# Attention scores of a transformer block: the keys' lo products on all 128 rows for short key ranges

## The chip, the cores and the metric

One core of a Trainium2 chip runs one program with a single launch. The metric is the device time of the program in microseconds, as the median of several runs. The engines of the core work side by side, each through its own queue in order: TensorE (PE, matmuls; PEld is its weight load), VectorE (DVE), ScalarE (ACT), GpSimd (POOL) and SyncE (SP, here for DMA alone).

## The reference, cut to what matters

The reference is one layer of a transformer block over 1024 tokens with a model width of 1024: a norm, a mixer of two attention branches (A and B), a second norm and a mixture of 32 experts. All of it is float32. The change touches the attention scores, of which there are three that matter here, all with head width 64 and eight query heads:

```python
s = einsum('bthd,btkd->bthk', q, ks) * scale        # branch A: 256 selected keys per query, one key head
s = einsum('btkgd,btksd->btkgs', qr, ks) * scale    # branch B, selected blocks: two key heads
s = einsum('btkgd,bskd->btkgs', qr, kw) * scale     # branch B, window of 512 keys
p = masked_softmax(s, mask)
```

Sixteen blocks of 64 keys are chosen out of sixteen in the second one, so it is causal attention over all keys. The kernel computes the first one over all causal keys too, with a bias that masks what isn't selected.

## The kernel before, in words

The kernel works in stages one behind another: norm and projections, with the index scores and their top 256 (0 to 474 us), attention (474 to 812), the merge and output projection with the router, and the experts with the final norm (both together 812 to 1429).

**Operands.** The score matmuls take operands of the type fp32r, so each float32 operand is split into a hi part and a lo part (the value minus its hi part). Of a query tile of 128 tokens, `q` holds for every head the 64 rows of the hi part and the 64 rows of the lo part in the 128 partitions: hi in partitions 0 to 63 and lo in 64 to 127 for a head of place x = 0, the other way round for x = 1 (lines 603 to 611). The keys `kk` hold the hi part (index 0) and the lo part (index 1), each twice: in partitions 0 to 63 and again in 64 to 127 (lines 620 to 635).

**A stage** (`stage`, line 896) is one query tile i of one of the three branches: selected blocks (`slc`), window and A. Its key range is n = (i - j0 + 1) x 128 keys; j0 is 0, in the window stage max(0, i - 4). There are 24 stages and eight small ones for compressed keys (`cmp_stage`). The query tiles go in the order 2, 3, 7, 6, 5, 1, 4, 0 (line 67).

**The scores of a pair of heads** (`score(h)`, for h and h + 1 as x = 0 and 1) go into PSUM tiles `s2` (in the trace `s`): one for both heads if n is at most 512, one for each otherwise, with two buffers. A range over 512 is cut in two: at 384 if n is 640, else at 512. The *first products* (line 929) multiply the 128 partitions of `q` by the hi part of the keys: hi x hi plus lo x hi at once. The *second products* (line 935) add hi x lo: for x = 0 they take partitions 0 to 63 of `q` and of the lo keys, for x = 1 partitions 64 to 127. They are half the array each, on different rows of it, and the loop puts the two heads side by side for each cut. `behind` (line 868) adds an ordering edge, without a semaphore, so that each of these matmuls comes right in the order written; the first of the second products stands behind the last of the first ones.

**What follows a pair.** VectorE adds the mask, negates and takes the row minimum (lines 944, 945, 952), ScalarE makes the exponential with its sum (953), VectorE the reciprocal (956) and POOL the scaling (960). In the next stage's time, `product(j)` turns the probabilities by PE transposes (971), VectorE or ScalarE copies them out (866), and `av` multiplies them by the values (879, 883): two matmuls of 64 output partitions side by side, half of the array's columns each.

**The order.** The loop at line 1058 issues the scores of a stage between the products of the stage before it. The program is scheduled by a planner (line 1692, `schedule_with_timeline_sim=True`): it places each engine's instructions by its own estimate of times, within the data dependencies and the edges added by hand.

Of the kernel before, what the change touches and what calls it, by code (L numbers as in the profile page):

```python
# [20 lines left out]
P = 128  # L21
# [80 lines left out]
def emit(tc, A):  # L102
# [366 lines left out]
    with ExitStack() as pi:  # L469
# [8 lines left out]
        def keys(g):  # L478

            ts_ = slice(g, g + G)  # L480
            src = kraw[:, ts_].rearrange("p t (a b) -> p t a b", a=2)
            out = ip.tile(tb, F32, name="qr")
            dve.tensor_tensor(ra, src, cos[:, ts_, None, ::2].to_broadcast(tb), op=OP.mult)
            dve.tensor_tensor(rb, src, sin[:, ts_, None, ::2].to_broadcast(tb), op=OP.mult)
            dve.tensor_tensor(out[:, :, 0], ra[:, :, 0], rb[:, :, 1], op=OP.subtract)
            dve.tensor_tensor(out[:, :, 1], ra[:, :, 1], rb[:, :, 0], op=OP.add)
            ks = ip.tile([P, G, 2, 2, 32], F32R, name="ks")
            kb = out.rearrange("p t a b -> p t (a b)")
            for x in range(2):
                act.activation(ks[:, :, x, 0], kb, AF.Copy)  # L490
            for x in range(2):
                dve.tensor_tensor(ks[:, :, x, 1], kb, f32(ks[:, :, x, 0]), op=OP.subtract)

            def turn():
                tr = ps1.tile([P, 512], F32, name="tr", bufs=2)
                for t in range(G):
                    pe.transpose(r32(tr[:, t * P:(t + 1) * P]), ks[:, t].rearrange("p a b c -> p (a b c)"), identr)
                dve.tensor_copy(kist[:, g * P:(g + G) * P], tr)
            return turn
# [188 lines left out]
    with ExitStack() as pk:  # L688
# [6 lines left out]
        with ExitStack() as pt:  # L695
# [77 lines left out]
            for t in range(2, NT):  # L773
                n = (t + 1) * P
# [14 lines left out]
            with tc.If(fv > 0):  # L789
                for t in range(2, NT):  # L790
                    n = (t + 1) * P
# [38 lines left out]
    with ExitStack() as pa:  # L830
# [32 lines left out]
        def flat(tr, n):  # L863
            ev[0] += 1
            h = ap_.tile([P, 512], F32, name="pth", bufs=NPT)
            return h[:n], (act.copy if EV[ev[0] % len(EV)] else dve.tensor_copy)(h[:n], tr[:n])  # L866

        def behind(i, j, sync=False):

            cl = mybir.DependencyClass  # L870
            tc.add_manual_dep(i.ins, j.ins.name, mybir.DependencyInfo(cl.Sync if sync else cl.NoSync, mybir.DependencyReason.DATA),
                              reason="side by side")
# [14 lines left out]
        def place(h):  # L887

            return h // 4 * 4 + h % 2 * 2 + h % 4 // 2
# [6 lines left out]
        def stage(i, q, keys, j0, gate, masked, vidx, avf, first, last, win=False):  # L896

            n = (i - j0 + 1) * P

            fold = win and i >= 4 and FOLD  # L900
            n_ = n - P if fold else n
            pgs = {}
            st = {}

            def score(h):

                g, hh = divmod(h, 4)
                if hh == 0:
                    st[g] = (ap_.tile([P, 4], F32, name="nm", bufs=4), ap_.tile([P, 4], F32, name="sm_", bufs=4))
                nm, sm_ = st[g]  # L910
                kk = keys(h)

                cut = 384 if n == 640 else 512
                s2s = []
                for x in range(2):

                    if n_ > 512 or x == 0:
                        pg = ap_.tile([P, S], F32, name="pg", bufs=NPG)
                    if n > 512 or x == 0:
                        s2 = ps2.tile([P, 1024], F32, name="s2", bufs=2)  # L920
                    o_ = 512 * x if n <= 512 else 0
                    p0 = 512 * x if n_ <= 512 else 0
                    pgs[h + x] = pg[:, p0:p0 + n_]
                    s2s.append(s2[:, 512 - cut + o_:])
                cs = [(c, w_) for c, w_ in ((0, min(n, cut)), (cut, n - cut)) if w_ > 0]
                mm = None
                for x in range(2):
                    for c, w_ in cs:
                        mm_, mm = mm, pe.matmul(s2s[x][:, c:c + w_], q()[:, place(h + x)], kk[:, 0, j0 * P + c:j0 * P + c + w_], start=True, stop=False)
                        if mm_:  # L930
                            behind(mm, mm_)
                for c, w_ in cs:
                    for x in range(2):
                        r = slice(64 * x, 64 * x + 64)
                        mm_, mm = mm, pe.matmul(s2s[x][:, c:c + w_], q()[r, place(h + x)], kk[r, 1, j0 * P + c:j0 * P + c + w_], start=False, stop=True)
                        behind(mm, mm_)

                mask = bias[:, soff[i]:soff[i] + n] if masked else window if win and i >= 4 else causal[:, S - n:]
                if fold:
                    fr = ap_.tile([P, 2, P], F32, name="fr", bufs=1)  # L940
                    nf = ap_.tile([P, 2], F32, name="nf", bufs=2)
                    for x in range(2):
                        y = hh + x
                        dve.tensor_tensor_reduce(fr[:, x], s2s[x][:, :P], mask[:, :P], -1.0, 3e38, op0=OP.add, op1=OP.min, accum_out=nf[:, x:x + 1])
                        dve.tensor_tensor_reduce(pgs[h + x], s2s[x][:, P:n], mask[:, P:], -1.0, 3e38, op0=OP.add, op1=OP.min, accum_out=nm[:, y:y + 1])
                        dg = pgs[h + x][:, n_ - P:]
                        dve.tensor_tensor(dg, dg, fr[:, x], op=OP.min)
                    dve.tensor_tensor(nm[:, hh:hh + 2], nm[:, hh:hh + 2], nf, op=OP.min)
                for x in range(2):
                    pg, y = pgs[h + x], hh + x  # L950
                    if not fold:
                        dve.tensor_tensor_reduce(pg, s2s[x][:, :n], mask, -1.0, 3e38, op0=OP.add, op1=OP.min, accum_out=nm[:, y:y + 1])  # L952
                    act.activation(pg, pg, AF.Exp, bias=nm[:, y:y + 1], scale=-1.0, accum_out=sm_[:, y:y + 1])  # L953
                if h % NB == NB - 2:
                    hb = hh - NB + 2
                    dve.reciprocal(sm_[:, hb:hh + 2], sm_[:, hb:hh + 2])
                    for x in range(NB):
                        h_ = h - NB + 2 + x
                        g2 = 1.0 if gate is None else gat[:, i, gate * 8 + h_:gate * 8 + h_ + 1]
                        pool.tensor_scalar(pgs[h_], pgs[h_], sm_[:, hb + x:hb + x + 1], g2, op0=OP.mult, op1=OP.mult)  # L960

            def product(j):
                pts = []
                both = fold and j == i

                def transposes():
                    c = n_ - (i - j + 1) * P
                    for g in range(2):
                        tr = ps2.tile([P, 512], F32, name="tr", bufs=3)
                        for hh in range(4):  # L970
                            pe.transpose(tr[:, hh * P:(hh + 1) * P], pgs[4 * g + hh][:, c:c + P], ident)  # L971
                        if both:
                            for x in range(2):
                                h = ap_.tile([P, 512], F32, name="pth", bufs=NPT)
                                pts.append((h, dve.tensor_tensor(
                                    h.rearrange("p (a q) -> p a q", a=4), tr.rearrange("p (a q) -> p a q", a=4),
                                    parts[:, x:x + 1].to_broadcast([P, 4, P]), op=OP.mult)))
                        else:
                            pts.append(flat(tr, P))

                def matmuls():
                    if both:
                        av(avf(), lambda g: vidx(g, j0), pts[1::2], False, False)
                        av(avf(), lambda g: vidx(g, j), pts[::2], False, last)
                    else:
                        av(avf(), lambda g: vidx(g, j), pts, first and j == j0, last and j == i)
                return transposes, matmuls, pts

            return ([lambda h=h: score(h) for h in range(0, 8, 2)], [product(j) for j in range(j0 + (1 if fold else 0), i + 1)])

        def cmp_stage(i, q, avf):
# [704 lines left out]
```

## Time and profile before

| | |
|---|---|
| median of 3 runs | 1431.48 us (1431.32 to 1436.68) |
| profiled execution | 1430.88 us |
| its span, first to last instruction | 1429.0 us |
| PE busy | 1332.3 us, 93% of the span |
| VectorE busy | 939.4 us, 66% |
| ScalarE busy | 700.6 us, 49% |
| POOL busy | 492.2 us, 34% |
| mean granted TensorE clock | 0.972 |

Busy times of matmuls overlap, since a matmul begins before the one ahead of it has left the array, and their ends are modelled. What one matmul costs its queue is read from the distance between two starts.

### The profile page before, as it was taken

How to read it: one execution, taken by the hardware profiler on the slowest of the kernel's cores; microseconds unless marked ns; L12 is line 12 of the kernel's file. 1: busy time of each engine (PE TensorE's matmuls, PEld its weight loads, DVE VectorE, ACT ScalarE, POOL GpSimd, SP SyncE). 2: the span in 40 equal slices, each digit the busy share in tenths (PEclk: the TensorE clock that was granted, in tenths of full speed). 3: DMA queues.
4: the chain of work that ended last, by engine and by line, in shares of the span. 5: the costliest groups of instructions: out<-in, count | busy, mean ns of one | idle time of the engine just before them, and what ended most of it. 6: DMA issues, size and time to landing. Idle time of an engine off the chain costs nothing. (4 is left out here: it accounts for less than half of the span.)

```text
span 1429.0 us, 21436 instructions
## 1 busy us (share of the span) xinstructions
PE 1332.3 (93%) x7095; PEld 999.3 (70%) x7095; DVE 939.4 (66%) x2335; ACT 700.6 (49%) x1452; POOL 492.2 (34%) x572
## 2 busy tenths in 40 slices
PE   4989999999999999999999999999689999898993
PEld 3889999988888655555565588877466667566662
DVE  7884778689600576677776696556766767565656
ACT  5513677622211575565576652222366656455554
POOL 3223777822312554444464400000132232233213
PEclk9999999999999999999999999999889999999996
DMA  6321443223333110101020274685689997699874
GB/s 202 80 63 59 143 131 107 79 83 103 91 94 111 45 53 8 45 16 30 19 72 16 60 230 140 197 305 180 221 292 296 326 325 237 199 327 316 300 235 179
DMA packets 126646, 214.82 MB, mean 150 GB/s; under 512 B 23081, under 2 KB 62033, under 8 KB 126530
## 3 DMA queue, kind: packets, MB, share of 16 engines
q1 hardware_dynamic: 110754, 174.53, 37.0%
q0 software_dynamic: 13680, 33.52, 8.6%
q10 hardware_dynamic: 2096, 5.36, 1.0%
q8 instruction: 57, 0.93, 0.3%
q14 instruction: 59, 0.48, 0.1%
HBM read 180.38 MB, written 49.28 MB: 161 GB/s over the span
## 5 line engine op out<-in xcount | busy, mean ns | idle before, releaser
L953 ACT ACTIVATE pg<-pg,nm 128x512 f32<-128x512 f32 (+7 forms) x192 | 138.9, 726 | 47.3 <-DVE nm L952 35.8
L221 PE MATMUL pj<-wh,hTl 128*128 128x288 f32 (+1 forms) x512 | 152.7, 299 | 7.8 <-DVE hTl L377 7.8
L219 PE MATMUL pj<-wh,hTh 128*128 128x288 f32 (+1 forms) x512 | 152.9, 299 | 1.9 <-DVE rb L260 1.0
L220 PE MATMUL pj<-wl,hTh 128*128 128x288 f32 (+1 forms) x512 | 152.0, 297 | 1.1 <-DVE wl L189 1.1
L189 POOL TENSOR_TENSOR wl<-wr,wh 128x512 fp32r<-128x512 f32 (+1 forms) x60 | 80.9, 1360 | 167.4 <-ACT wh L188 165.8
L971 PEld LDWEIGHTS tr<-ident,pg 128*128 128x128 f32 x784 | 84.9, 142 | 61.4 <-issue 30.3
L971 PE MATMUL tr<-ident,pg 128*128 128x128 f32 x784 | 115.6, 283 | 1.3 <-ACT pth L866 1.2
L220 PE MATMUL u<-gl,xh 128*128 128x512 f32 x256 | 112.6, 440 | 2.5 <-DVE gl L1432 2.5
L1471 POOL DMA_INDIRECT acc<-y,lis x30 | 55.7, 1858 | 161.0 <-ACT y L1465 106.9
L219 PE MATMUL u<-gh,xh 128*128 128x512 f32 x256 | 107.9, 422 | 2.2 <-ACT gh L1431 1.5
L221 PEld LDWEIGHTS pj<-wh,hTl 128*128 128x128 f32 x512 | 97.7, 191 | 9.6 <-DVE hTl L377 9.1
L221 PE MATMUL u<-gh,xl 128*128 128x512 f32 x256 | 103.3, 403 | 0.0
L1432 DVE TENSOR_TENSOR gl<-cr,gh 128x1024 fp32r<-128x1024 f32 x68 | 81.5, 1221 | 32.0 <-ACT gh L1431 24.3
L219 PE MATMUL pj<-hTh,wh 128*128 128x512 f32 x256 | 101.2, 395 | 0.0
L221 PE MATMUL pj<-hTh,wl 128*128 128x512 f32 x256 | 101.1, 395 | 0.0
L220 PE MATMUL pj<-hTl,wh 128*128 128x512 f32 x256 | 100.8, 394 | 0.0
L219 PEld LDWEIGHTS pj<-wh,hTh 128*128 128x128 f32 x512 | 98.1, 192 | 3.3 <-ACT hTh L376 1.3
L220 PEld LDWEIGHTS pj<-wl,hTh 128*128 128x128 f32 x512 | 97.8, 191 | 2.4 <-DVE wl L189 1.6
L866 DVE COPY pth<-tr 128x512 f32<-128x512 f32 (+1 forms) x102 | 69.8, 687 | 42.8 <-PE tr L971 36.1
L866 ACT COPY pth<-tr 128x512 f32<-128x512 f32 (+1 forms) x102 | 58.5, 580 | 66.2 <-PE tr L971 38.1
L1432 DVE TENSOR_TENSOR gl<-ck,gh 128x1024 fp32r<-128x1024 f32 x55 | 66.7, 1222 | 35.8 <-PE u L220 20.3
L1431 ACT ACTIVATE gh<-cr 128x1024 fp32r<-128x1024 f32 x68 | 70.2, 1062 | 17.4 <-DMA cr<-in_w_gate_up 8.2
(590 smaller groups left out, 3432.8 us busy)
## 6 DMA issues: line engine op xcount, KB each, us to landing
cr<-in_w_gate_up SPq DMA_DIRECT2D x68, 512.0 KB
ck<-in_w_gate_up SPq DMA_DIRECT2D x55, 512.0 KB
cr<-in_w_down SPq DMA_DIRECT2D x32, 512.0 KB
ck<-in_w_down SPq DMA_DIRECT2D x30, 512.0 KB
wr<-in_w_in SPq DMA_DIRECT2D x48, 256.0 KB
qscr<-qTs SPq DMA_DIRECT2D x96, 128.0 KB
q<-qscr POOLq DMA_DIRECT2D x24, 512.0 KB, 3.7
xt<-in_x SPq DMA_DIRECT2D x16, 512.0 KB
```

Source lines behind the costliest of these rows:

```text
L189: eng.tensor_tensor(lo[:, k:k + 2, w], raw[:, :, w], f32(hi[:, k:k + 2, w]), op=OP.subtract)
L219: pe.matmul(ps, lh, rh, start=first, stop=False)
L220: pe.matmul(ps, lh, rl, start=False, stop=False)
L221: pe.matmul(ps, ll, rh, start=False, stop=last)
L866: return h[:n], (act.copy if EV[ev[0] % len(EV)] else dve.tensor_copy)(h[:n], tr[:n])
L953: act.activation(pg, pg, AF.Exp, bias=nm[:, y:y + 1], scale=-1.0, accum_out=sm_[:, y:y + 1])
L971: pe.transpose(tr[:, hh * P:(hh + 1) * P], pgs[4 * g + hh][:, c:c + P], ident)
L1431: act.activation(gh, w, AF.Copy)
L1432: dve.tensor_tensor(gl, w, f32(gh), op=OP.subtract)
L1471: pool.indirect_dma_start(out=acc[:], out_offset=bass.IndirectOffsetOnAxis(ap=idx, axis=0), in_=y, in_offset=None, compute_op=OP.add, boun ...
```

## The change

For key ranges of at most 640 keys (five key tiles), the second products take all 128 partitions of `q` and of the lo keys. They compute hi x lo plus lo x lo, where before the lo x lo part was left out. They are full-array matmuls then, and the ordering edge ahead of each of them is left out. For n above 640 nothing is changed. The number of matmuls is the same.

```diff
+                short = n <= 640
                 for c, w_ in cs:
                     for x in range(2):
-                        r = slice(64 * x, 64 * x + 64)
+                        r = slice(0, P) if short else slice(64 * x, 64 * x + 64)
                         mm_, mm = mm, pe.matmul(s2s[x][:, c:c + w_], q()[r, place(h + x)], kk[r, 1, j0 * P + c:j0 * P + c + w_], start=False, stop=True)
-                        behind(mm, mm_)
+                        if not short:
+                            behind(mm, mm_)
```

## Rows read from the trace of the kernel before

**Rows 1.** Windows: stretch, busy us (x instructions) of PE, PEld, DVE, ACT, POOL; clock, DMA, GB/s.

```profile
474.00:486.00 12.00, 9.47 (x44) 5.35 (x44) 9.34 (x36) 10.27 (x29) 6.57 (x10) 0.89 0.14 45
...
715.00:738.00 23.00, 22.13 (x144) 14.36 (x143) 17.14 (x68) 18.50 (x62) 19.86 (x34) 1.00 0.27 83
...
787.00:812.00 25.00, 25.00 (x165) 15.56 (x165) 15.86 (x73) 16.34 (x60) 14.89 (x30) 1.00 0.09 24
...
1050.00:1400.00 350.00, 336.40 (x1360) 228.80 (x1358) 227.35 (x265) 201.91 (x295) 101.65 (x63) 0.99 0.87 287
```

**Rows 2.** PE's waits, 474 to 812 us: us in total, times, longest us.

```profile
PE s L929 <- DVE nm L952: 6.3, 9, 1.1
```

**Rows 3.** Timeline of PE, 512 keys: start us, us, engine, line, op, out<-in, shapes, xcount.

```profile
505.80 0.71 PE L929 MATMUL s<-kB,q 128*128 128x512 f32 x2
506.44 0.51 PE L935 MATMUL s<-kB,q 64*128 64x512 f32 x2
506.88 0.66 PE L971 MATMUL tr<-ident,pg 128*128 128x128 f32 x4
507.46 0.64 PE L879 MATMUL av<-pth,vB 128*64 128x512 f32 x1
```

**Rows 4.** Timeline of PE, 512 keys, transposes between first and second products.

```profile
500.09 0.71 PE L929 MATMUL s<-kB,q 128*128 128x512 f32 x2
500.64 0.60 PE L971 MATMUL tr<-ident,pg 128*128 128x128 f32 x4
501.17 0.50 PE L935 MATMUL s<-kB,q 64*128 64x512 f32 x2
```

**Rows 5.** Timeline of PE in the projections: full matmuls of 512 and of 256 columns.

```profile
400.35 0.39 PE L219 MATMUL pj<-hTh,wh 128*128 128x512 f32 x1
400.58 0.39 PE L220 MATMUL pj<-hTl,wh 128*128 128x512 f32 x1
...
451.93 0.28 PE L220 MATMUL pj<-wl,hTh 128*128 128x256 f32 x1
452.05 0.28 PE L221 MATMUL pj<-wh,hTl 128*128 128x256 f32 x1
```

**Rows 6.** Timeline of PE, 384 keys.

```profile
495.34 0.44 PE L935 MATMUL s<-kA,q 64*128 64x384 f32 x2
495.71 0.55 PE L971 MATMUL tr<-ident,pg 128*128 128x128 f32 x3
```

**Rows 7.** Timeline of PE, 256 keys.

```profile
719.13 0.38 PE L935 MATMUL s<-kB,q 64*128 64x256 f32 x2
719.45 0.44 PE L971 MATMUL tr<-ident,pg 128*128 128x128 f32 x2
```

**Rows 8.** Timeline of PE, 640 keys (384 and 256 columns, merged under the first shape).

```profile
743.39 0.83 PE L929 MATMUL s<-kB,q 128*128 128x384 f32 x4
744.15 0.56 PE L935 MATMUL s<-kB,q 64*128 64x384 f32 x4
744.64 0.66 PE L971 MATMUL tr<-ident,pg 128*128 128x128 f32 x4
```

**Rows 9.** Timeline of PE, 128 keys.

```profile
795.61 0.42 PE L929 MATMUL s<-kB,q 128*128 128x128 f32 x2
795.95 0.33 PE L935 MATMUL s<-kB,q 64*128 64x128 f32 x2
796.21 0.66 PE L971 MATMUL tr<-ident,pg 128*128 128x128 f32 x4
```

**Rows 10.** Timeline of PE, 512 keys, value products behind the pair.

```profile
503.09 0.50 PE L935 MATMUL s<-kB,q 64*128 64x512 f32 x2
503.52 0.64 PE L879 MATMUL av<-pth,vB 128*64 128x512 f32 x1
```

**Rows 11.** Timeline, 640 keys: [idle us before it <- releaser].

```profile
560.46 0.56 PE L929 MATMUL s<-kB,q 128*128 128x384 f32 x2 [0.58 <-DVE nm L952]
...
561.54 0.29 DVE L944 CUSTOM_DVE_ANT_0 fr<-s,window 128x128 f32<-128x128 f32 x1 [0.53 <-PE s L935]
```

## The prediction

> **What bounds the kernel now.** I read the page's engine table first: TensorE (PE) is the busiest engine by far, and the diff touches the attention stage alone (474 to 812 us), so I asked for the busy times of that stage cut at its query tiles. The reader is to see two kinds of stretch. In the last one, query tile 0, PE is busy 25.00 of 25 us while VectorE has 15.86 and POOL 14.89; in query tile 1 it is 22.13 of 23, with POOL close behind at 19.86. In the first one, PE is busy only 9.47 of 12 and VectorE 9.34 [rows 1]. A busy PE may still stand in a queue of its own, so the view of PE's waits comes next: over the whole stage its largest entry is 6.3 us for VectorE's row minimum, nine waits, because a new score tile must wait until VectorE has read the old one [rows 2]. Nothing else is large. So attention goes at the pace of TensorE's own instructions, except in a few places where VectorE sets it. The third view is the timeline of PE alone, read by the distance from one start to the next. The ends of matmuls are modelled; their starts give the slots.
>
> **What a pair costs today.** At four key tiles (512 keys) two first products start at 505.80, the half-array pair at 506.44, transposes at 506.88 and the next operation at 507.46 [rows 3]. So 0.64 us for two full products, 0.44 for the pair, 0.58 for four transposes. Elsewhere the same two full products are followed by transposes and not by half-array work: 500.09 to 500.64 is 0.55, and those four transposes take 0.53, to 501.17 [rows 4]. Hence entering the half-array pair costs 0.09 us, and coming back to transposes 0.05. A plain full product of 512 columns in a run takes 0.23 (400.35 to 400.58), one of 256 columns 0.12 (451.93 to 452.05) [rows 5]. The 0.55 is then 2 x 0.23 plus a lead of 0.09, which the first product has in both versions. The pair itself, 0.44, is hardly shorter than two plain products, 0.46: both halves start together, but nothing else runs beside them.
>
> **The change part by part.** It adds no DMA, no wait, no instruction. For n up to 640 the two second products of a head pair become full-array matmuls; 18 of the 24 stages are short, with four head pairs each, so 72 pairs: 12 each at 128, 256, 384 and 512 keys and 24 at 640 (window stages of tiles 5 to 7, all three of tile 4). Per pair followed by transposes, or by the next first products, the saving is: the entry (0.09), plus the pair minus the plain products that replace it, plus the return (0.05).
> - 512 keys: 0.09 + 0.44 - 0.46 + 0.05 = 0.12.
> - 384: the pair takes 0.37 [rows 6]. A plain product of 384 comes out of the 640 case, where four first products take 0.76 [rows 8]: less the lead and the entry, and less two of 256, 0.17 remain for each. 0.09 + 0.37 - 0.34 + 0.05 = 0.17.
> - 256: the pair takes 0.32 [rows 7]; 0.09 + 0.32 - 0.24 + 0.05 = 0.22.
> - 640: two pairs in a row take 0.49 (744.15 to 744.64) [rows 8] against 0.58 for four plain products; 0.09 - 0.09 + 0.05 = 0.05.
> - 128: 0.34 for the first products and 0.26 for the pair [rows 9]. A plain product of 128 in a run isn't shown. Taking lead and entry from the 0.34 leaves 0.08 each; 0.12 (the slot of 256) is the other end. Before is 0.34 + 0.26 + 0.05 = 0.65; after is 0.09 + 4 x 0.08 = 0.41 to 0.09 + 4 x 0.12 = 0.57: a saving of 0.08 to 0.24. I take a slot of 0.10, between the ends, and 0.16.
>
> Where the value products (av, half the columns, two side by side) follow, the entry and return don't go away, they move: the array must be regrouped for av anyhow, and the half-array pair hands over to av in the same 0.43 (503.09 to 503.52) [rows 10]. There only pair minus plain products is left: -0.02 at 512, +0.03 at 384, +0.08 at 256, -0.09 at 640, about +0.02 at 128. In the timeline nine pairs stand ahead of av: 2 at 512, 1 at 384, 1 at 256, 1 at 640, 4 at 128.
>
> Thirteen pairs stand where VectorE sets the pace or the clock is low: 7 at 384 at the start, where the granted clock is 0.89 of full over the stretch [rows 1], 1 at 256, 5 at 640. PE's saving there is worth between nothing (VectorE is late next) and the full 7 x 0.17 + 0.22 + 5 x 0.05 = 1.66; I take half, 0.83.
>
> The sum over the others: 128: 8 x 0.16 + 4 x 0.02 = 1.36; 256: 10 x 0.22 + 0.08 = 2.28; 384: 4 x 0.17 + 0.03 = 0.71; 512: 10 x 0.12 - 2 x 0.02 = 1.16; 640: 18 x 0.05 - 0.09 = 0.81. Together 6.32, with the paced ones 7.15, so 7.2 us. The ends of the 128 term (eight pairs by 0.08 either way) and of the paced pairs put it at 5.7 to 8.6.
>
> The ordering edges between second products go too. The planner then sets these matmuls where its own costs put them; the trace before cannot show that order. One more change of grouping around an av pair costs 0.14 (entry and return); one saved gains as much. With some fifteen moved either way that is 2 us to both sides; I take none.
>
> Does it reach the end? After attention PE is again the fullest engine: 336.40 of 350 us in the expert stage, where DMAs are busy 0.87 of the time [rows 1]. Those weight loads go into buffers that PE's work frees, so they begin earlier by the same amount; I count the saving whole. The profiled execution took 1430.88 us (1429.0 span and 1.9 around it), 0.6 below the median of the runs, 1431.48. From the median, 1431.5 - 7.2 = 1424.3.
>
> **A rule that speaks against it.** The trace shows 0.44 us for the lone pair at 512 [rows 3]. The Trainium skill, "TensorE: Matmul & The Clock Gate", Part 3 ("Measured speedup vs the span model"), says that matmuls on different row groups together last as long as one matmul plus some 4 ns for each further one. By that the pair would be worth 0.23, and the change would add a whole stream of columns for each pair, some 14 us in all; the lone pairs of this trace don't bear that out. It is the second rival below, there worked out from rows alone.
>
> **The rivals.**
> 1. *The saved time turns into waits.* In query tile 1 POOL is busy 19.86 of 23 us and PE would save 2.3 of them; at tiles 0 and 2 each stage is a short chain score, minimum, exponential, normalise, transpose. If VectorE, ScalarE or POOL catch up there, the 256 and half of the 128 terms are lost, 3 us: gain 4.2, so 1427.3. For it: the POOL row. Against it: PE 25.00 of 25 in tile 0 with all others under two thirds [rows 1].
> 2. *The cost of a pair is not the change of grouping.* Each pair has overhead beyond one stream of its columns: at 512, 0.09 + 0.44 - 0.23 + 0.05 = 0.35, at the other sizes much the same; 72 x 0.34 is 24.5 us. If it comes from the second product as such (adding to a PSUM tile just written), full-array products keep it, and the added streams must be paid: 12 x (0.10 + 0.12 + 0.17 + 0.23) + 24 x 0.29 = 14.4 us. With a quarter of the overhead gone it ends at 1431.5 + 14.4 - 6.1 = 1440. It decides for slower as soon as less than 0.6 of the overhead goes. Against it: first products that follow one another in one tile group show neither the 0.09 nor the 0.21 [rows 4, 5].
> 3. *More than the sum.* With the edges gone, the second product of head x = 0 no longer stands behind the first product of x = 1. Where the latter waits for its score tile, VectorE waits too: at 640 keys PE waited 0.58 us at 560.46 for x = 1, and VectorE then sat idle 0.53 until the half-array products ended [rows 11]. x = 0 could be ready before that. Given back at about half a microsecond in six or seven such places, this adds 3 us to the 7.2. In the first stretch, where PE stood idle a fifth of the time, the granted clock is 0.89; less idling might leave it at the upper of its two levels, 2.4 GHz, for longer. I put the whole at 10.5, 1421.
> 4. *It does nothing.* The planner takes the freed time for another order that loses as much: 1431.
>
> **How the numbers follow.** About 0.5%, 7.2 us, is what a measurement of this kernel can tell from no change, so faster is below 1424.3 and slower above 1438.6. The forecast, 1424.3 with its own range 1422 to 1427, has 0.50, and its lower half is faster by that bound: 0.25. Rival 1 has 0.17 (same), rival 2 0.08 (slower), rival 3 0.20 (faster), rival 4 0.05 (same). Faster 0.45, same 0.47, slower 0.08. The range that holds 8 in 10 runs from below rival 3 to past rival 4: 1416 to 1433; it leaves out rival 2 and the far end of rival 3.
>
> **What would show it.** In the changed timeline the four products of a head pair should take 0.09 + 4 x 0.23 = 1.01 at 512 keys instead of 1.08 (505.80 to 506.88 [rows 3]) and 0.57 at 256, and four transposes behind them 0.53 instead of 0.58. The half-array rows of the 72 pairs are gone, with starts 0.12 to 0.23 apart in their place. Attention should end some 7 us earlier with PE's waits unchanged. If the new starts are 0.2 or more apart at 256 columns, rival 2 is right; if slots shrink and the waits for VectorE or POOL grow, rival 1; if the waits for VectorE at 640 keys shrink, rival 3. The prediction is wrong if attention ends within 3 us of where it did, or more than 12 earlier.

## The result, and the profile after

The changed kernel takes 1407.89 us (median of 4 runs, 1407.07 to 1410.02) against 1431.97 (4 runs) for the kernel before: a ratio of 0.9827, 95% interval 0.9803 to 0.9851, or 24 us less. Forecast were 7.2 us less, 1424.3. Attention, from its first compressed product to the start of its last value product, went from 341.1 us (473.9 to 815.0) to 318.3 (473.6 to 791.9). That is nearly all of it: what follows attention takes 613.9 us before and 613.3 after.

The engine table of the changed kernel's page: TensorE's matmuls (PE) are less busy by 17.5 us and its weight loads (PEld) busier by 9.5; VectorE, ScalarE and POOL are within 1.5 us of where they were.

```profile
PE 1314.8 (94%) x7095; PEld 1008.8 (72%) x7095; DVE 939.7 (67%) x2335; ACT 699.1 (50%) x1452; POOL 492.9 (35%) x572
```

In the changed kernel the second products are line 937, the transposes 974, the row minima 947, 948 and 955. First the slots, from its timeline of PE: 512, 256 and 128 keys.

```profile
497.80 0.71 PE L929 MATMUL s<-kB,q 128*128 128x512 f32 x2
498.35 0.63 PE L937 MATMUL s<-kB,q 128*128 128x512 f32 x2
498.81 0.60 PE L974 MATMUL tr<-ident,pg 128*128 128x128 f32 x4
...
704.17 0.48 PE L929 MATMUL s<-kB,q 128*128 128x256 f32 x2
704.49 0.40 PE L937 MATMUL s<-kB,q 128*128 128x256 f32 x2
704.73 0.40 PE L929 MATMUL s<-kB,q 128*128 128x256 f32 x2
...
768.17 0.42 PE L929 MATMUL s<-kB,q 128*128 128x128 f32 x2
768.43 0.39 PE L937 MATMUL s<-kB,q 128*128 128x128 f32 x2
768.65 0.29 PE L974 MATMUL tr<-ident,pg 128*128 128x128 f32 x1
```

From start to start, the four products at 512 keys take 498.81 - 497.80 = 1.01, against 1.08 in [rows 3], and at 256 keys 0.56: the predicted 1.01 and 0.57. (A slot is the distance from one start to the next.) A full product of 128 columns has a slot of 0.22 / 2 = 0.11, where 0.10 was taken. So the pieces are as predicted. Yet the gain is three times their sum; what else has gone is in the waits and the clock.

PE's waits after, 474 to 812 us (us in total, times, longest us):

```profile
PE s L929 <- DVE nm L955: 3.0, 4, 1.1
...
PE s L929 <- DVE nm L948: 0.3, 1, 0.3
```

The first answers to [rows 2], 6.3 us in nine waits. The windows show where the waits were and a second thing that went with them. These are the kernel before and then the changed one (columns as in [rows 1]):

```profile
548.00:572.00 24.00, 20.48 (x94) 11.33 (x92) 15.31 (x50) 12.38 (x26) 12.18 (x12) 0.86 0.00 0
...
760.00:790.00 30.00, 27.51 (x170) 16.05 (x170) 21.32 (x73) 18.55 (x45) 11.34 (x15) 1.00 0.06 19
```

```profile
474.00:486.00 12.00, 8.97 (x50) 6.89 (x50) 9.97 (x38) 10.52 (x31) 6.99 (x11) 1.00 0.16 46
548.00:572.00 24.00, 23.74 (x148) 15.26 (x145) 19.63 (x63) 15.28 (x34) 11.68 (x13) 1.00 0.08 23
760.00:790.00 30.00, 30.00 (x202) 19.19 (x200) 19.77 (x82) 20.46 (x71) 16.00 (x32) 1.00 0.09 27
1026.00:1376.00 350.00, 335.93 (x1363) 228.25 (x1362) 227.74 (x264) 202.68 (x294) 101.26 (x63) 1.00 0.87 287
```

Between 548 and 572 us, PE was idle for 3.5 us of 24 and the granted clock was 0.86; after, it is idle for 0.26 and the clock is 1.00, and 148 matmuls stand where 94 did (not the same work, since the stages begin at other times). In the first stretch (474 to 486 us) the clock went from 0.89 [rows 1] to 1.00, though PE stood idle for 3.03 of the 12 us, against 2.53 before. The expert stage is unchanged against [rows 1] (335.93 for 336.40), only 24 us earlier.

To split the gain, every distance from one PE start to the next in attention was set against the median distance for the same operation, columns and neighbours over the traces of this case. The medians are "slots", what stands over them by more than 0.15 us is "waits", and the surplus in stretches at the 1.2 GHz level is "half clock". Between 0.8 and 3.2 us of small differences remain over, so the parts don't add up to the whole quite. Another way of taking the medians moves the first two columns by about 1 us, and waits against half clock by 2 us in the last row; the column "attention" is read from two starts and depends on no median. All in us, attention alone, from one profiled execution of each kernel. The last column counts how often PE goes from one grouping of the array to another (half-array second products, value products, all else). The rows between the first and the changed kernel, and the last one, are the experiments told below.

| kernel | slots | waits | half clock | attention | switches |
|---|---|---|---|---|---|
| before | 319.6 | 15.6 | 3.8 | 341.1 | 305 |
| full products, order of before held | 311.1 | 17.9 | 2.7 | 334.9 | 170 |
| half products, order of the next line held | 318.1 | 11.1 | 2.9 | 334.1 | 301 |
| full products, all edges kept | 309.6 | 12.9 | 0 | 325.7 | 167 |
| full, edges kept, head by head | 309.7 | 6.2 | 0 | 318.3 | 168 |
| changed kernel | 309.7 | 6.1 | 0 | 318.3 | 168 |
| half products, edges dropped | 334.0 | 8.2 | 6.8 | 349.8 | 343 |

The change saved 9.9 us of slots, 9.5 of waits and 3.8 of half clock. Read down the column "attention", it is a chain of three steps: full products in the old order save 6.2 us, the new order that the planner makes of them 9.2 more, and the dropped edges another 7.4.

### The profile page after: what moved, and what is told of

Same layout as the page of the kernel before. It is cut to its first block, busy times and chain, and to the rows that moved or that the text cites. A ratio compares the mean times of both kernels' runs of the same rounds, so it can differ in the third digit from the quotient of the medians.

```text
span 1405.3 us, 21446 instructions
## 1 busy us (share of the span) xinstructions
PE 1314.8 (94%) x7095; PEld 1008.8 (72%) x7095; DVE 939.7 (67%) x2335; ACT 699.1 (50%) x1452; POOL 492.9 (35%) x572
## 5 line engine op out<-in xcount | busy, mean ns | idle before, releaser
L974 PE MATMUL tr<-ident,pg 128*128 128x128 f32 x784 | 111.5, 278 | 0.6 <-ACT pth L866 0.6
```

## The experiments

Ratios are against the kernel before, run in the same batch on the same chip, where it had medians of 1434.1, 1431.0 and 1430.8 us in the three batches.

**1. Full products, every edge kept** (full_edges).

```diff
-                        r = slice(64 * x, 64 * x + 64)
+                        r = slice(0, P) if n <= 640 else slice(64 * x, 64 * x + 64)
```

> Second products of short pairs on all 128 rows, all ordering edges kept. Theory 1 (the dropped edge does most: x = 0 no longer waits behind the first products of x = 1): only the slots gain, some 8 to 10 us, about 1423, and the waits for VectorE in attention (9 us of PE's before) stay. Theory 2 (the shorter slots do it all, the edges nothing): about 1408, as the changed kernel.

Measured: 1415.26 us, 0.9863 (0.9835 to 0.9891), which neither theory expected. By the medians the array form alone gives about 19 us and some 5 of the change's 24 are left for the dropped edges; by attention alone it is 15.4 and 7.4. The interval, 4 us to either side, allows both. In attention, the waits fell from 15.6 to 12.9 and the half clock from 3.8 to nothing, though not one edge was touched: the planner put PE's instructions in another order. Nothing but the form of these products differs in the text. Whether the planner prices a full one otherwise than a half one, or sees other dependencies because a full one reads all 128 rows of the keys, no run here shows.

**2. Half products as before, the edges dropped** (half_noedge).

```diff
-                        behind(mm, mm_)
+                        n <= 640 or behind(mm, mm_)
```

> Second products of short pairs stay half the array each, but without their ordering edges. Theory 1: the waits go, 10 to 13 us, but halves that no longer stand side by side cost a stream and two changes of grouping each: 1420 to 1430. Theory 2: nothing to gain, torn pairs cost: 1432 or more.

Measured: 1439.95 us, 1.0042 (1.0019 to 1.0065), slower by 0.4%. The number is theory 2's, the mechanism theory 1's: the waits fell by 7.5 us to 8.2, nearly as they did between full_edges and the changed kernel (6.8), but the slots grew by 14.4. The reason is in the timeline of PE at 640 keys:

```profile
622.49 0.54 PE L929 MATMUL s<-kB,q 128*128 128x384 f32 x2
622.96 0.56 PE L935 MATMUL s<-kB,q 64*128 64x384 f32 x2
623.44 0.56 PE L929 MATMUL s<-kB,q 128*128 128x384 f32 x2
623.94 0.55 PE L935 MATMUL s<-kB,q 64*128 64x384 f32 x2
624.42 0.77 PE L971 MATMUL tr<-ident,pg 128*128 128x128 f32 x5
```

The two heads' half-array products no longer stand side by side: each head's two run alone. The eight products take 1.93 us (622.49 to 624.42) against 1.25 in [rows 8]; all 24 pairs at 640 keys are torn in this trace, and no other pair is; at 0.6 to 0.7 each they are the 14.4. So the edges had a purpose while the products were half-array ones, and cost something once they are full.

**3 and 4. The change at up to 512 keys only, and at 640 keys only** (le512, only640).

```diff
-                short = n <= 640
+                short = n <= 512        # le512
+                short = n == 640        # only640
```

> The change at up to 512 keys only (48 pairs); 640 keys as before. Theory 1 (the edge matters where each head of the pair has a score tile of its own, at 640 keys): the slots alone, 5.5 to 7 us, about 1426. Theory 2 (shorter slots): most of the gain too, since the slots at 640 keys save only 0.05 us a pair: 1410.

> The change at 640 keys only (24 pairs). Theory 1: 14 to 17 us, about 1416, with the waits of the stretches at 557 to 577 and 738 to 787 us gone. Theory 2: the slots, 24 x 0.05, so 1431.

Measured: 1414.58, 0.9871 (0.9844 to 0.9898), and 1425.39, 0.9935 (0.9914 to 0.9957), each between its two theories. In attention le512 has 9.2 us less of slots than before, 3.0 less of waits and 2.2 less of half clock; only640 has 1.7 less of slots, 4.0 less of waits and as much half clock as before. Predicted were 5.5 us of slots for the four short sizes (6.9 with the paced pairs in full) and 0.8 to 1.1 for 640, so the short sizes do bring most of them, and more than predicted. Most of the 640 gain is waits.

**5. Full products, in the order of before** (full_set). Every instruction of attention on PE, VectorE, ScalarE and POOL is kept by name and put behind the one that it followed in the kernel before. The wrapper that keeps them gives all of them line 112 in the profile.

```diff
+    made = {}
+    pe, dve, act, pool = (Kept(e, made) for e in (pe, dve, act, pool))
...
-                        r = slice(64 * x, 64 * x + 64)
+                        r = slice(0, P) if n <= 640 else slice(64 * x, 64 * x + 64)
...
+        for names in SET_ORDER:
+            for n0, n1 in zip(names, names[1:]):
+                behind(made[f"I-{n1}"], made[f"I-{n0}"])
```

> Second products of short pairs on all 128 rows, and every engine's instructions of the attention stage held in the order of the kernel before by ordering edges. Theory A (three parts: shorter slots, another order that the planner makes of full-array products, and the dropped edges): only the slots are left, some 10 us, and the waits of before (4 us at the window stage of tile 7, 4 us at tile 4) stay: about 1422 against 1432. Theory B (shorter slots alone take the waits away, in any order): as with full rows and the old edges, about 1415.

Measured: 1421.89 us, 0.9936 (0.9915 to 0.9957), 9 us less, as theory A expected. This is the change as the prediction saw it: shorter slots, the same order. All 1944 matmuls of attention stand in the trace in the sequence that they had before. The slots gave 8.5 us, 2.3 came back as waits, and attention is 6.2 shorter. The other 3 lie behind attention, where two profiles of the changed kernel alone differ by 3.9 (613.3 and 609.4). Between 715 and 738 us, where query tile 1 was before, the same instructions take 1.8 us less and PE's idle time among them is unchanged, 0.87 us; the waits that came back are in the first stretch (2.53 us idle before, 3.41 now) and at tile 7. There the old bad stretch still stands, in the window of full_set:

```profile
548.00:572.00 24.00, 20.23 (x95) 13.02 (x95) 14.70 (x49) 12.01 (x25) 12.65 (x12) 0.86 0.00 0
```

**6. Half products, in the order of full_edges** (half_full_order). The counterpart: the diff of experiment 5 without the edit of `r`, and with the list of names read from full_edges.

> Half-array second products as before, all 72 pairs intact, but attention's instructions on PE, VectorE, ScalarE and POOL are held, by ordering edges, in the order that the planner chose for full rows with all edges kept (full_edges, 1415). Theory O (the new order is a gain of its own, about 9 us, since it removes the waits of tile 7 and the stretch at half clock, whatever form the products have): 1431.5 - 9 = 1422, and no half-clock stretch at 560 to 570 us. Theory F (the order only fits the shorter slots of full products; with half-array ones the same waits appear): 1428 to 1434. In either case attention should keep the switches between array groups of before.

Measured: 1423.16 us, 0.9941 (0.9922 to 0.9959), 7.6 us less with not one product changed, as theory O expected. The order is worth that much by itself. The two parts multiplied, 0.9936 x 0.9941 = 0.9877, account for full_edges within its interval (0.9835 to 0.9891). In attention alone they are 6.2 and 7.0 us of 15.4; the rest is about the size of the half clock below, 2.9 us, which full_edges doesn't have. Cut at the first compressed product of each query tile, the new order shows in two tiles only: tile 7 takes 67.0 us before and 61.9 here (with full products 67.3 and 61.8), tile 2 25.1 and 23.1 (23.4 and 19.8). The six others take the same in both orders within 0.1 us. Of the expectation, the missing half clock at 560 to 570 came true too:

```profile
474.00:492.00 18.00, 15.66 (x72) 9.51 (x71) 13.45 (x49) 14.05 (x40) 11.19 (x17) 0.81 0.19 60
...
548.00:572.00 24.00, 23.84 (x148) 14.20 (x146) 18.64 (x61) 15.76 (x35) 11.06 (x12) 1.00 0.07 22
```

The stretch at half clock at 483 us, which full_edges doesn't have, is longer here than before (to 490.2 us instead of 486.7; 0.81 in the window) and costs 2.9 us. So the two stretches at half clock have different grounds. The one near 483 us goes with the form: the four traces with half products at tile 2 have it, the ten with full ones don't, in whatever order. The one near 560 us goes with the order of before: full_set has it, half_full_order doesn't. What the new order does at tile 7 can be read off two timelines of PE. The kernel before:

```profile
557.25 0.74 PE L935 MATMUL s<-kB,q 64*128 64x512 f32 x4
557.92 0.44 PE L971 MATMUL tr<-ident,pg 128*128 128x128 f32 x2
559.32 0.56 PE L929 MATMUL s<-kB,q 128*128 128x384 f32 x2 [0.96 <-DVE nm L952]
...
562.59 1.69 PE L929 MATMUL s<-kB,q 128*128 128x384 f32 x4 [1.08 <-DVE nm L945]
...
566.66 1.42 PE L929 MATMUL s<-kB,q 128*128 128x384 f32 x4
```

and half_full_order (first and second products have one line there, so they merge):

```profile
556.79 0.54 PE L112 MATMUL s<-kB,q 128*128 128x384 f32 x2
557.25 1.94 PE L112 MATMUL av<-pth,vA 128*64 128x512 f32 x8
559.12 0.66 PE L112 MATMUL tr<-ident,pg 128*128 128x128 f32 x4
559.53 1.02 PE L112 MATMUL s<-kB,q 128*128 128x384 f32 x6
560.49 1.53 PE L112 MATMUL tr<-ident,pg 128*128 128x128 f32 x12
561.77 0.54 PE L112 MATMUL s<-kB,q 128*128 128x384 f32 x2
562.47 1.02 PE L112 MATMUL s<-kB,q 128*128 128x384 f32 x6 [0.16 <-DVE nm L112]
```

Before, the score products of tile 7's window come with little between them, and PE waits until VectorE has read a score tile: 0.96 us, then the 0.58 of [rows 11], then 1.08. All value products of the stage ahead had been started before 556.42. In the new order eight of them (1.87 us) stand between a first product and its next, and PE doesn't wait when it comes back.

**7. Head by head, every edge kept** (head_by_head, and head_again). The order that dropping the edges allows is written out: both products of x = 0, then both of x = 1.

```diff
-                for x in range(2):
-                    for c, w_ in cs:
...
-                for c, w_ in cs:
-                    for x in range(2):
...
+                hi = lambda x, c, w_: pe.matmul(...)    # first product, as before
+                def lo(x, c, w_):                       # second product, on slice(0, P) if short
...
+                if short:
+                    seq = [(f, x, c) for x in range(2) for f in (hi, lo) for c in cs]
+                else:
+                    seq = [(hi, x, c) for x in range(2) for c in cs] + [(lo, x, c) for c in cs for x in range(2)]
+                for f, x, c in seq:
+                    mm_, mm = mm, f(x, *c)
+                    if mm_:
+                        behind(mm, mm_)
```

> Full rows, with all ordering edges, but written head by head: first and then second products of x = 0, then of x = 1. Theory A1 (what the dropped edges give is that x = 0 is ready before the score tile of x = 1 is free): as the changed kernel, about 1408, and the waits at tile 4 gone. Theory A2 (what they give is the planner's freedom to put other work between): no better than with the old edges, about 1415.

> Head by head at up to 640 keys with all edges kept, once more, beside the changed kernel on the same chip. Theory A1 (the whole gain of dropping the edges is that x = 0 no longer stands behind x = 1; writing that order out gives the same): 1405 to 1409 and within 3 us of the changed kernel. Theory A2 (freedom for the planner matters by itself): more than 4 us behind it.

> The changed kernel itself, beside the others on the same chip: 1408, within 2 us.

Measured: 1405.25, 0.9822 (0.9793 to 0.9850); again 1404.74, 0.9817 (0.9795 to 0.9839), beside 1406.78, 0.9827 (0.9807 to 0.9846) for the changed kernel itself in that batch. This is theory A1 both times. Waits and slots are those of the changed kernel to 0.1 us, and all 1944 matmuls of attention stand in its sequence. So the freedom given to the planner is worth nothing beyond the order that it led to; the worth is in x = 0 not standing behind x = 1. Tile 4 shows it best, with 5.1 of the 7.4 us (52.0 us in full_edges, 46.9 in the changed kernel). Tile 4 in full_edges, timeline of PE:

```profile
749.16 0.53 PE L929 MATMUL s<-kB,q 128*128 128x384 f32 x2
749.53 0.38 PE L971 MATMUL tr<-ident,pg 128*128 128x128 f32 x2
749.98 0.53 PE L929 MATMUL s<-kB,q 128*128 128x384 f32 x2
750.35 0.75 PE L935 MATMUL s<-kB,q 128*128 128x384 f32 x4
750.94 0.38 PE L971 MATMUL tr<-ident,pg 128*128 128x128 f32 x2
752.08 0.53 PE L929 MATMUL s<-kB,q 128*128 128x384 f32 x2 [0.76 <-DVE nm L945]
```

and in the changed kernel:

```profile
743.25 0.54 PE L929 MATMUL s<-kB,q 128*128 128x384 f32 x2
743.63 0.46 PE L937 MATMUL s<-kB,q 128*128 128x384 f32 x2
743.92 0.46 PE L929 MATMUL s<-kB,q 128*128 128x384 f32 x2
744.22 0.45 PE L937 MATMUL s<-kB,q 128*128 128x384 f32 x2
744.60 0.64 PE L879 MATMUL av<-pth,vc 64*64 64x512 f32 x1
```

With the edges, the second products of x = 0 start at 750.35 or later, 1.2 us behind its first ones at 749.16; VectorE gets both tiles late and the next pair waits 0.76. Head by head, x = 0's second products start 0.38 behind its first ones, and no wait for VectorE is left in this stretch. Of the ranges up to 640 keys only 640 itself can gain this way by the program's text: below it, both heads share one score tile. The traces agree: le512 drops the edges below 640 keys alone, and in the tiles that have only such ranges (2, 3, 1 and 0) it takes the times of full_edges, 19.8, 31.6, 17.9 and 27.1 us.

**8 to 10. Full products for longer ranges** (all_full, le768; and head_all, which is head_by_head with the same edit).

```diff
-                short = n <= 640
+                short = True            # all_full, head_all
+                short = n <= 768        # le768
```

> The change for every key range. Slots: pairs above 640 keys have 0.09 + 0.33 + 0.32 + 0.05 against 0.92 at 1024 keys, so 0.13 us lost for each of 8 pairs, 0.07 at 896, about nothing at 768: 1.6 us slower than the changed kernel, 1409.5, if slots decide. If the freedom of order decides, some us faster than it, 1403 to 1406.

> The change up to 768 keys. By the slots as the changed kernel, 1408 (8 pairs at 0.0 to 0.02 us each). If the freedom of order at two score tiles decides, 1 to 3 us faster.

> Full rows for every key range, and first and second products head by head for every key range, with all ordering edges. Theory A (it is the sum of slots, and of x = 0 being ready early): over 640 keys a full row costs what it cost in all_full, -1 to +2 us against the limit at 640, and x = 0 early gains some tenths in six stages of tile 6 and 7: 1403 to 1407. Theory B (the planner's order is what decides, and is drawn anew by any change of the text): anywhere from 1400 to 1415, not told apart from chance.

Measured: 1406.9, 0.9832 (0.9805 to 0.9860); 1409.76, 0.9843 (0.9813 to 0.9873); 1407.02, 0.9823 (0.9799 to 0.9847). None can be told from the changed kernel, so the expected 1.6 us of all_full can't be confirmed either. Attention takes 318.3, 321.9 and 318.3 us, against 318.3; le768, which the planner put in another order, is the longest. No version that was run beats the changed kernel by more than the intervals.

## Why the prediction was right in its parts and wrong in the sum

- **The slots: right.** 1.01 and 0.56 us where 1.01 and 0.57 were forecast. The prediction put all slots together at 6.32 + 1.66 = 8.0 us; with the order held they gave 8.5. By stretches, waits included: 1.15 us between 500 and 533 us for the 512 keys (forecast 1.16), 1.84 at tile 1 (2.3), 1.42 at tile 0 (1.36).
- **The paced pairs: right in kind.** Half of 1.66 was struck off for VectorE; in the held order 2.3 us of slots came back as waits. 6.2 us net in attention stand against the forecast 7.15. Rival 1 (the saved time turns into waits) is this in kind, but not where it was placed: no wait for POOL appeared at tile 1.
- **The step that failed: "The planner then sets these matmuls where its own costs put them ... With some fifteen moved either way that is 2 us to both sides; I take none."** The order was priced by its switches of array grouping, and the runs show that this is not where its price lies: the new order has about as many switches with half products (301 for 305). What it changes is which waits exist, and with them the half clock at tile 7. It is worth 7.6 us with the products untouched, about as much as the slots, and 9.2 us of attention once they are full; and it came from the array form, not from the dropped edges to which the sentence ties it. The dropped edges brought a further 7.4 us of attention, by the next point. Rival 4 had the planner's new order lose as much as the slots gain; it gained instead.
- **Rival 3: the mechanism right, the size less than half.** x = 0 ready ahead of x = 1 was put at "half a microsecond in six or seven such places", 3 us. The waits fell by 6.8 us between full_edges and the changed kernel and by 7.5 between the kernel before and half_noedge. It belonged into the sum and not among the rivals: the 0.53 us of idle VectorE in [rows 11] showed it directly, and 24 pairs have 640 keys. Its remark on the clock came true, but not by less idling: up to 483 us, where the clock fell before, PE is idle for 2.63 us now and was for 2.31.
- **"Nothing else is large": too quick.** The view of PE's waits in the kernel before names 6.3 us [rows 2], and four smaller rows beside it:

```profile
PE s L929 <- DVE nm L945: 2.7, 3, 1.1
PE tr L971 <- ACT pth L866: 1.2, 2, 0.6
PE av L879 <- ACT pth L866: 0.3, 1, 0.3
PE tr L1024 <- POOL pc L1016: 0.2, 1, 0.2
```

  Measured by the distances between starts, PE's waits in attention were 15.6 us and the half clock 3.8. That is 19.4 us which an order could give back, and the bound of the order term should have been that, on the side of a gain. With it the range would have reached to about 1431.5 - 8.0 - 19.4 = 1404.
- **The rest held.** What follows attention took the gain whole (613.9 and 613.3 us). Rival 2 fell: the second product as such carries no overhead, since two full ones of 512 columns take 0.46 us (498.35 to 498.81), as two plain ones do. (Its "less than 0.6 of the overhead" is the point of no change; to end above its own bound for slower, 1438.6, less than 0.3 would have had to go.) The Trainium skill, "TensorE: Matmul & The Clock Gate", Part 3 ("Measured speedup vs the span model"), gives the time that matmuls on different row groups last together, with some 4 ns for each further one. The trace agrees as far as that goes: the two of [rows 3] start at 506.439 and 506.443 us. But this is how long the pair lasts, and not what it costs PE's queue: 0.44 us to the next start, where a plain product costs 0.23. So the streams of columns that the prediction's estimate would add don't follow from it for a lone pair between full-array work; held in the same order, the change made attention shorter by 6.2 us.

Not settled: why the planner's estimate gives the better order for full products. Only its outcome was run, in a few orders; another could be better or worse. Why the clock near 483 us goes with the form of the products is open too.

## What to carry to other kernels

Where a planner orders the work, a change of an instruction's form can be two changes: its slots, which the rows of the trace gave here to within 1 us in all, and a new order. What an order won here came from the waits and the low-clock time in the stage, 19.4 us in all, so they, and not the number of instructions moved, are the measure of what one can win; what it can lose isn't bounded by them (half_noedge lost 14.4 us of slots). Sum the waits from the distances between starts before putting the order at nothing. To tell the two apart, hold the old order with the new form and the new order with the old form; here they gave 9.1 and 7.6 us, together 16.7 of the 19 of both at once.

## What the runs showed of the hardware that was not expected

- Half-array products that have lost their partner are dear. At 640 keys, two products of one head (384 and 256 columns) on half the rows take 0.48 us alone (623.94 to 624.42), as much as all four of both heads side by side, 0.49 [rows 8].
- A busy PE can stay at the lower clock for long. In half_noedge PE had waited twice for VectorE shortly ahead of 562 us, 0.95 us before 559.32 and 0.46 before 561.98; then the granted clock lay at 0.50, the 1.2 GHz level, for 17 us (562.1 to 579.2) in which PE was never idle by the profile. The timeline of PE and the window of that kernel:

```profile
559.32 0.56 PE L929 MATMUL s<-kB,q 128*128 128x384 f32 x2 [0.95 <-DVE nm L952]
...
561.98 0.72 PE L929 MATMUL s<-kB,q 128*128 128x384 f32 x2 [0.46 <-DVE nm L945]
```

```profile
562.00:579.00 17.00, 17.00 (x50) 9.81 (x51) 9.22 (x44) 7.04 (x18) 8.71 (x9) 0.50 0.10 32
```

  The kernel before does the same work up to 559.8, had waited 0.96 and 0.58 us there, and lay at that level from 561.8 to 568.6, with a third wait of 1.08 us inside. What prolongs it no run here shows. In the changed kernel, which has only a wait of 0.3 us there, the clock doesn't fall in attention at all.
- The lower clock doesn't follow idle time alone. From 474 to 483 us PE is idle for 2.63 us in the changed kernel, and the granted clock stays at 1.00 throughout attention; in the kernel before it is idle for 2.31, and the clock falls at 483.3 (0.89 from 474 to 486 us, [rows 1]).
